# The exact rest of streamed weights, by a subtraction on VectorE or by an accumulating DMA

## The chip, the cores and the metric

The kernel runs on one core of one Trainium2 chip. The metric is the device time of one execution in microseconds (us); lower is better. A second number, the span, is the time from the first to the last instruction in one profiled execution.

## The reference

One layer of a hybrid decoder works on 512 prompt tokens and 32 sample tokens (8 sequences of 4), 1024 channels wide. After an RMSNorm comes one input projection for seven parts. A diagonal state-space branch (S5) and a gated linear recurrence (HGRN2, 8 heads) run side by side and are merged by sigmoid gates; then an output projection, and an MLP with a squared ReLU, each with norms around it:

```python
h = rms_norm(x, norm_mix_pre)
proj = h @ w_in + b_in                                   # 1024 -> 6656
u, q, f, i, g, gate_s5, gate_hg = jnp.split(proj, SPLIT_POINTS, axis=-1)
y_s5, s5_re, s5_im = s5_mixer(u, ...)
y_hg, hg_s = hgrn2_mixer(q, f, i, g, ...)
merged = jax.nn.sigmoid(gate_s5) * (y_s5 @ w_br_s5) + jax.nn.sigmoid(gate_hg) * (y_hg @ w_br_hg)
x = x + rms_norm(merged @ w_out, norm_mix_post)
h2 = rms_norm(x, norm_mlp_pre)
m = jnp.square(jax.nn.relu(h2 @ w_up)) @ w_down          # 1024 -> 4096 -> 1024
x = x + rms_norm(m, norm_mlp_post)
```

All inputs are fp32. The outputs are the tokens and the final states of both branches.

## The kernel before, in words

Channels lie on the 128 partitions, tokens along the rows: 544 tokens as two halves of 272. A dense product is done in three passes over fp32r operands: each operand is cut into a high part (11 bits of mantissa) and the exact rest, and TensorE sums high x high, high weight x rest of the activation, and rest of the weight x high. `dense` (L106) does this for one column tile of 128 outputs: per block k of 128 input channels it issues three pairs of matmuls, the two halves of the tokens each, in the order wh·xh, wh·xl, wl·xh. A tile of 8 blocks is 48 matmuls and reads weights of 128 x 1024 words (512 KB); a tile of w_down has 7 blocks, 42 matmuls and 128 x 896 words (448 KB).

`weights` (L83) brings in such a tile. SP's queue loads the fp32 words into wt (three buffers), ScalarE copies them into wh, which rounds them (L97), and VectorE subtracts wh from wt into wl (L98; as it goes through the helper tt, the profile shows it as L69). wh and wl have two buffers each in the pool wp. Where a caller passes a pool as `res`, the two parts get places of their own there and stay: four column tiles of w_out and four of w_up, which are used by halves of the tokens. Everything else is streamed: column tiles come in, are used once and make room. In the profile a streamed tile carries its matrix's name: wt_in, wh_in, wl_in for the input projection, _bh and _bs for the branches, _gl for the gated linear unit, _o for the output projection, _u and _d for the MLP.

The order of TensorE's work up to the branches is written out by hand: column tiles of the input projection are cut into blocks (`dense_steps`, class Fill) and put between the matmuls of the HGRN2 cores, the S5 tables and the S5 scan, a few blocks at a time. From about 530 us the kernel is mainly one column tile after another: gated linear unit, S5 branch, output projection, then the MLP in three parts (14 + 14 + 4 tiles of w_up; after each of the first two, 8 x 2 tiles of w_down). The last tiles of the output projection and the first of w_up are done by halves of the tokens, and the last 512 rows of w_down (w_down2) are cut into two parts by `split` (L129), outside of `weights`.

The order on the other engines comes from a scheduler that places instructions as it expects them to become ready, by their place in the program less an offset: weights run ahead by 100 (WAHEAD), the emptying of PSUM by 50 (EAHEAD). The head (up to `make_masks()`, where the tiles 4 and 5 of w_in are loaded early) and the tail are ordered by hand on TensorE, ScalarE and VectorE. All engines and queues work in their order. POOL's queue carries the constants, S5's loads (U, PT, tab, Q, T, L890 to L898), the stores y_d (L962) and some memsets.

What empties PSUM after a column tile: in the input projection a sigmoid or a copy on ScalarE (L501, L520, L974), in w_up a ReLU on ScalarE and then a square on VectorE, a copy and a subtraction (`act_full`, L1164 to L1168), in w_down a copy on ScalarE in the first part (L1217) and an addition on VectorE in the second (L1219).

Of the kernel before, what the change touches and what calls it, by code (L numbers as in the profile page):

```python
# [9 lines left out]
F32 = mybir.dt.float32  # L10
# [10 lines left out]
NT = 544          # tokens: two halves of 256 prompt + 16 sample tokens  # L21
# [4 lines left out]
WAHEAD, EAHEAD = 100, 50     # how far weights and the emptying of PSUM run ahead in the schedule  # L26
# [13 lines left out]
def b2(ap, n):  # L40
    """[p, a] -> [p, a, n], the last axis repeated."""
    return ap.unsqueeze(2).to_broadcast([ap.shape[0], ap.shape[1], n])
# [3 lines left out]
def layer(ctx, tc, a, o):  # L46
    nc = tc.nc
# [35 lines left out]
    def weights(src, name, res=None, ahead=WAHEAD):  # L83
        """res: a pool in which the two parts stay."""
        n = 1
        for d in src.shape[1:]:
            n *= d
        if len(src.shape) == 3:
            src = src.rearrange("p a b -> p (a b)")
        elif len(src.shape) == 4:  # L90
            src = src.rearrange("p a b c -> p (a b c)")
        with tc.high_priority(offset=ahead):
            wt = wp.tile([P, n], F32, tag="wt", name=f"wt_{name}", bufs=3)
            nc.sync.dma_start(out=wt, in_=src)
            wh = (res or wp).tile([P, n], F32R, tag="wh", name=f"wh_{name}")
            wl = (res or wp).tile([P, n], F32R, tag="wl", name=f"wl_{name}")
            S.copy(wh, wt)  # L97
            tt(wl, wt, wh.bitcast(F32), SUB)  # L98
        return wh, wl
# [6 lines left out]
    def dense(ps, wh, wl, xs, first=True, last=True):  # L106
        """ps[:, half, :] (+)= sum_k W_k^T X_k; xs: per k the halves of the hi and the lo part."""
# [8 lines left out]
    def dense_half(ps, ws, xs, hf, ks=None):  # L116
        """ps[:, i, :] = sum_k W_ik^T X_k for two column tiles i and one half of the tokens; ks: these k alone."""
# [16 lines left out]
    gains = const("gains", q=nc.gpsimd)        # [128, 4, 8]  # L134
    lg = const("lb_logits", q=nc.gpsimd)

    def rstd(r, q2, ps):
        """r = 1/sqrt(ps/1024), good to the last bits; ps: 1024 * (mean of squares + eps)."""
        S.activation(r, ps, AF.Abs_reciprocal_sqrt, bias=zero_t, scale=1.0 / 1024)
        S.activation(q2, r, AF.Square)  # L140
        stt(q2, ps, -0.5 / 1024, q2, MUL, MUL)
        stt(r, q2, 1.5, r, ADD, MUL)
# [67 lines left out]
    bmask = const("bmask", q=nc.gpsimd)          # [128, 8]  # L210
    hgn = const("hg_norm", q=nc.gpsimd)          # [128, 1]

    def hq(t):
        """[p, 2, 544] in halves -> prompt [p, 2, 256], sample [p, 2, 16]; t: [p, 2, >=272]"""
        return t[:, :, 0:256], t[:, :, 256:HT]

    def tq(t):
        """[p, 544] prompt first, sample last -> the same two views"""
# [13 lines left out]
    # the input and what goes into S5 lie where the next groups' tiles will  # L232
# [10 lines left out]
    # ---- first norm and the S5 input, half of the tokens after half; the input goes through DRAM to be laid out by  # L243
    # (step in chunk, channel) ----
# [11 lines left out]
    def sums0(hf):  # L256
# [3 lines left out]
        # each of 128 partitions adds its share of 1024 eps  # L260
# [67 lines left out]
    # lower bound of the forget gate: softmax over the two rows, first row  # L328
# [34 lines left out]
    with tc.manual_schedule(engines={ET.PE, ET.Activation, ET.DVE, ET.SP}):  # L363
        # the tensor engine's clock comes up while the first loads are under way
# [77 lines left out]
    def inproj(m):  # L442
        """One column tile of the input projection; yields after each of its 8 blocks of rows."""
# [12 lines left out]
    class Fill:  # L456
        """Column tiles that go into the tensor engine's stream a few blocks at a time, between other work."""
# [19 lines left out]
    # blocks of column tiles between the parts of the S5 tables, the HGRN2 cores and the S5 scan  # L477
    F1, F2, F3, FL, FK, FO, FN, FH, FY, FD, FS = 44, 1, 32, 5, 4, 2, 3, 22, 3, 12, 2

# [1 line left out]
    def hgrn_in(g, gp):  # L481
        """The tiles of a group of two heads and what fills them."""
# [42 lines left out]
    def hgrn_core(g, T, hp, scT, scS):  # L525
        """Scores inside windows of 128 tokens (4 for samples), level by level: blocks of 2h tokens, queries of the
        upper half against keys of the lower. qp: q times the decay since its block of h began; k: k times the decay
        until its block ends; tots: the decay of whole blocks. All factors are at most 1."""
# [10 lines left out]
        def lv(t, h, n):  # L539
            """blocks of 2h tokens as [p, d, n, 2, h], or with (d n) as one axis"""  # L540
# [7 lines left out]
        # token-major values and keys  # L548
# [25 lines left out]
        def sample_tokens():  # L574
            # samples: four copies of the 32 tokens along the rows, cut so that one pass sums all partial products
# [35 lines left out]
        for L in range(7):  # L611
# [19 lines left out]
            # on to blocks of 2h  # L631
# [25 lines left out]
        # states after each window, and the outputs  # L657
# [15 lines left out]
        for i in range(2):  # L673
            # token by token, so that the norm's sums run along the rows
# [12 lines left out]
        # the samples' outputs lie feature by feature  # L687
# [37 lines left out]
    y_d = dp.tile([8, 16, 32, 72], F32, tag="y_d", name="y_d")  # L725

    def cmul(e, outr, outi, xr, xi, yr, yi, t, conj=False):
        """out = x * y (or its conjugate); out aliases neither."""
# [21 lines left out]
    def s5_parameters(sp):  # L750
        """Per state: decay and rotation of a step and of a chunk, and the input coefficient."""
# [7 lines left out]
        # decay per step and per chunk of 8 steps; rotation per 1, 8, 16, .., 256 steps  # L759
# [31 lines left out]
        # input coefficient (A - 1) / a  # L791
# [12 lines left out]
    def s5_tables(sp, keep):  # L804
        """The large tables, which depend on the parameters alone, into DRAM."""
# [8 lines left out]
        # -Im C, and C in blocks for pairs of groups  # L814
# [11 lines left out]
        # rotation tables  # L826
# [18 lines left out]
        # the response inside a chunk  # L845
# [12 lines left out]
        # what a chunk adds to the state  # L858
# [10 lines left out]
        # read-out of the state t+1 steps on  # L869
# [12 lines left out]
    def s5_late(sp, keep):  # L882
# [3 lines left out]
        for hf in range(2):  # L886
# [25 lines left out]
            # sample states  # L912
# [17 lines left out]
            # the states before each chunk, for pairs of groups in blocks  # L930
# [9 lines left out]
            for c in range(4):  # L940
# [11 lines left out]
                # gelu: y * sigmoid(2 sqrt(2/pi) (y + 0.044715 y^3))  # L952
# [138 lines left out]
    def squares(acc, ps, name, first):  # L1091
        """acc += ps^2, [128, 2, n] each"""
# [8 lines left out]
    with tc.tile_pool(name="res", bufs=5, reuse_waits="tile") as rp:  # L1101
# [53 lines left out]
        def act_out(ps, dst, n):  # L1155
            """relu(ps)^2 into the two parts of each dst"""
# [13 lines left out]
        # relu(r x)^2 = r^2 relu(x)^2: the norm's factor r = 1/sqrt(v) is left out before the MLP; with it the  # L1170
        # last norm's 1/sqrt(mean + eps) is 1/sqrt(mean + eps v^2) of what comes out. e8: eps v^2, as what
        # each of 128 partitions adds to the sum over 1024 channels
# [20 lines left out]
    with tc.tile_pool(name="act", bufs=1, reuse_waits="tile") as apool:  # L1193
# [26 lines left out]
        # the last part's weights stay, in the place of activations that are done  # L1220
# [17 lines left out]
        def e_out(m, hf):  # L1238
            """Adds the parts, squares; the gain comes in after the squares."""
# [66 lines left out]
def kperm(w, k):  # L1306
    """[k*128, m*128] -> [m, 128, k, 128]"""
# [72 lines left out]
```

## Time and profile before

| | |
|---|---|
| median of 2 runs | 1028.97 us (1028.68 to 1029.27) |
| span of the profiled execution | 1027.5 us |
| instructions | 18826 |
| TensorE busy | 1010.4 us, 98% of the span |
| VectorE busy | 550.1 us, 54% |
| ScalarE busy | 399.9 us, 39% |
| POOL busy | 40.5 us, 4% |
| moved by the DMA queues | 107.27 MB, 104 GB/s on average |

The profiled execution is known by its span alone; the runs, timed without a profile, are 1.2 to 1.8 us above it. PE is TensorE's matmuls, PEld its weight loads (beside PE), DVE VectorE, ACT ScalarE, SP the queue that issues most DMAs. Matmuls overlap, so the length of one (288 ns) is more than the distance from one to the next; the pace of the stream is read from starts. PEclk is the granted clock as a share of full speed.

### The profile page before, as it was taken

Reading aid. Unit: us, or ns where it says so; the run is one execution under the profiler, and the core shown is the slowest. Engines: PE = TensorE matmul, PEld = TensorE weight load, DVE = VectorE, ACT = ScalarE, POOL = GpSimd, SP = SyncE. Lnnn points to the kernel's source line nnn. Section 1 sums busy time; section 2 is a strip of 40 time slices with the busy share of each in tenths; the row PEclk is TensorE's granted clock in tenths of the full one; section 3 lists DMA queues with packets and bytes.
Section 4 is the critical chain, followed back from the end, with each engine's and each line's share of the span. In section 5 each row is a group of like instructions: output and inputs, shape, how many; then the busy total and the mean of one; then the engine's idle time right before and its main releaser. Section 6 shows DMA issues by size and latency. Waiting matters only on the chain.

```text
span 1027.5 us, 18826 instructions
## 1 busy us (share of the span) xinstructions
PE 1010.4 (98%) x8032; PEld 993.7 (97%) x8032; DVE 550.1 (54%) x1006; ACT 399.9 (39%) x740; POOL 40.5 (4%) x77
## 2 busy tenths in 40 slices
PE   8999999999999999999999999999999999999995
PEld 6999999999999999999999999999999999999994
DVE  7856447466465496767547649445211344322357
ACT  6654254253442633344324546343222333211243
POOL 1100000000000000124110000000000000000000
PEclk9999899999999999999999999999999999999998
DMA  7431132131131243845452341122233222222312
GB/s 266 102 120 48 56 108 83 45 126 62 58 127 58 89 141 131 290 138 207 149 152 83 103 144 63 41 81 73 90 91 100 83 87 91 75 88 93 107 38 88
DMA packets 37796, 107.27 MB, mean 104 GB/s; under 512 B 8320, under 2 KB 11744, under 8 KB 37200
## 3 DMA queue, kind: packets, MB, share of 16 engines
q1 hardware_dynamic: 33440, 91.82, 27.8%
q0 software_dynamic: 3728, 13.68, 4.1%
q8 instruction: 63, 1.03, 0.4%
q10 hardware_dynamic: 544, 0.56, 0.2%
q14 instruction: 21, 0.17, 0.1%
HBM read 90.04 MB, written 14.83 MB: 102 GB/s over the span
## 4 chain that ended last, share of the span: by engine, by line
PE 95%; DVE 2%; ACT 1%; DMA 1%; SPq 0%; issue 0%; DVEq 0%; ACTq 0%
PE ps_in L114 27%; PE ps_d L114 16%; PE ps_u L114 15%; PE ps_u L124 7%; PE ps_bh L114 5%; PE psL L619 5%; PE ps_o L114 2%; PE ps_o L124 2%; PE ps_bs L114 2%; PE ps_e L124 2%; PE psOs L596 1%; PE psy L950 1%; DMA wt_in<-in_w_in 1%; PE psD L608 1%; PE psO L679 1%; PE psK L663 1%
## 5 line engine op out<-in xcount | busy, mean ns | idle before, releaser
L114 PE MATMUL ps_in<-hh,wh_in 128*128 128x272 f32 x736 | 159.8, 298 | 0.0
L114 PE MATMUL ps_in<-hh,wl_in 128*128 128x272 f32 x736 | 154.2, 291 | 0.0
L114 PE MATMUL ps_in<-hl,wh_in 128*128 128x272 f32 x736 | 154.1, 290 | 0.0
L114 PEld LDWEIGHTS ps_in<-hh,wh_in 128*128 128x128 f32 x736 | 117.0, 191 | 0.9
L114 PEld LDWEIGHTS ps_in<-hl,wh_in 128*128 128x128 f32 x736 | 117.1, 191 | 0.0
L114 PEld LDWEIGHTS ps_in<-hh,wl_in 128*128 128x128 f32 x736 | 116.8, 191 | 0.0
L69 DVE TENSOR_TENSOR wl_in<-wt_in,wh_in 128x1024 fp32r<-128x1024 f32 (+1 forms) x54 | 61.6, 1143 | 66.1 <-ACT wh_in L97 64.4
L97 ACT CAST wh_in<-wt_in 128x1024 fp32r<-128x1024 f32 x46 | 48.3, 1051 | 118.9 <-PE ps_in L114 105.0
L114 PE MATMUL ps_u<-zl,wh_u 128*128 128x272 f32 x416 | 86.3, 289 | 0.0
L114 PE MATMUL ps_u<-zh,wh_u 128*128 128x272 f32 x416 | 86.1, 288 | 0.0
L114 PE MATMUL ps_u<-zh,wl_u 128*128 128x272 f32 x416 | 86.0, 288 | 0.0
L69 DVE TENSOR_TENSOR wl_d<-wt_d,wh_d 128x896 fp32r<-128x896 f32 x32 | 35.0, 1092 | 93.8 <-ACT wh_d L97 93.7
L97 ACT CAST wh_d<-wt_d 128x896 fp32r<-128x896 f32 x32 | 30.1, 942 | 123.6 <-PE ps_d L114 113.2
L69 DVE TENSOR_TENSOR wl_u<-wt_u,wh_u 128x1024 fp32r<-128x1024 f32 x32 | 39.0, 1224 | 71.3 <-ACT wh_u L97 71.2
L114 PEld LDWEIGHTS ps_u<-zh,wh_u 128*128 128x128 f32 x416 | 65.4, 188 | 0.2
L114 PEld LDWEIGHTS ps_u<-zh,wl_u 128*128 128x128 f32 x416 | 65.4, 188 | 0.0
L114 PEld LDWEIGHTS ps_u<-zl,wh_u 128*128 128x128 f32 x416 | 65.1, 189 | 0.0
L97 ACT CAST wh_u<-wt_u 128x1024 fp32r<-128x1024 f32 x32 | 33.4, 1047 | 70.2 <-PE ps_u L114 46.6
L114 PE MATMUL ps_d<-a0l,wh_d 128*128 128x272 f32 x256 | 53.1, 289 | 0.0
L114 PE MATMUL ps_d<-a0h,wl_d 128*128 128x272 f32 x256 | 52.9, 288 | 0.0
L114 PE MATMUL ps_d<-a0h,wh_d 128*128 128x272 f32 x256 | 52.8, 288 | 0.0
L619 PE MATMUL psL<-qp,k 128*128 128x64 f32 (+2 forms) x448 | 52.1, 268 | 0.0
(477 smaller groups left out, 2129.6 us busy)
## 6 DMA issues: line engine op xcount, KB each, us to landing
wt_in<-in_w_in SPq DMA_DIRECT2D x52, 512.0 KB, 3.6
wt_u<-in_w_up SPq DMA_DIRECT2D x32, 512.0 KB, 3.4
wt_d<-in_w_down SPq DMA_DIRECT2D x32, 448.0 KB, 3.3
s<-in_hg_s SPq DMA_DIRECT2D x8, 512.0 KB, 4.9
out_hg_s<-s SPq DMA_DIRECT2D x8, 512.0 KB, 3.4
wt_bh<-in_w_br_hg SPq DMA_DIRECT2D x8, 512.0 KB, 3.5
wt_o<-in_w_out SPq DMA_DIRECT2D x8, 512.0 KB, 3.4
x<-in_x POOLq DMA_DIRECT2D x2, 1088.0 KB, 8.7
```

The lines of the kernel that those rows point to most:

```text
L69: (e or V).tensor_tensor(out=out, in0=x, in1=y, op=op)
L97: S.copy(wh, wt)
L114: mm(ps[:, i, 0:int(np.prod(x[i].shape[1:]))], lhsT=w[:, c], rhs=x[i], start=st, stop=sp)
L124: mm(ps[:, i, 0:HT], lhsT=ws[i][j][:, c], rhs=x[hf], start=st, stop=sp)
L596: mm(pos[:, 4 * b:4 * b + 4], lhsT=s0[:, b], rhs=qp[:, i, NP_ + 4 * b:NP_ + 4 * b + 4], start=False, stop=(b == 7))
L608: mm(pd[:, w], lhsT=k[:, i, c], rhs=q[:, i, c], start=True, stop=True)
L619: mm(pq[0:m, i, w * 64:(w + 1) * 64], lhsT=k[:, i, w * P:w * P + m], rhs=up(w * P, (w + 1) * P, i), start=True, stop=True)
L663: mm(pk[:, w], lhsT=kt2[:, i, w], rhs=vt[:, i, w], start=True, stop=True)
L679: mm(po[:, w], lhsT=sc[:, i, c], rhs=vt[:, i, w], start=True, stop=(w == 0))
L950: mm(py2[:, 72 * x_:72 * x_ + 72], lhsT=T.rearrange("p t c g -> p (t c) g")[:, :, 2 * gp_ + x_], rhs=U[:, 2 * gp_ + x_, 0:72], start=False ...
```

## The change

For streamed weights (no `res`) VectorE's subtraction goes. In its place ScalarE writes the negated high part into wl, and a DMA on POOL's queue reads the same weights from DRAM again and adds them onto wl, so that wl holds the weights less their high part. Resident weights keep the subtraction. Apart from this the diff only takes out comments.

```diff
             S.copy(wh, wt)
-            tt(wl, wt, wh.bitcast(F32), SUB)
+            if res is None:
+                S.activation(wl, wh.bitcast(F32), AF.Copy, scale=-1.0)
+                nc.gpsimd.dma_start(out=wl, in_=src, accum_op=ADD)
+            else:
+                tt(wl, wt, wh.bitcast(F32), SUB)
         return wh, wl
```

## Rows read from the trace of the kernel before

**Rows 1.** The page: span, and busy us, share and instructions of each engine.
```profile
span 1027.5 us, 18826 instructions
PE 1010.4 (98%) x8032; PEld 993.7 (97%) x8032; DVE 550.1 (54%) x1006; ACT 399.9 (39%) x740; POOL 40.5 (4%) x77
```
**Rows 2.** Stretches: length; busy us of PE, PEld, DVE, ACT, POOL; PEclk; DMA share; GB/s.
```profile
0.00:50.00 50.00, 46.39 (x297) 39.96 (x297) 37.72 (x125) 31.82 (x70) 7.23 (x24) 1.00 0.58 182
...
660.00:950.00 290.00, 290.00 (x2309) 289.84 (x2308) 96.07 (x108) 83.38 (x110) 0.00 (x0) 1.00 0.27 84
950.00:1027.50 77.50, 65.47 (x507) 63.84 (x506) 42.36 (x68) 28.68 (x51) 0.00 (x0) 0.95 0.24 77
```
**Rows 3.** Timeline of PE around tiles of w_up: start, length, engine, line, operation.
```profile
819.62 0.41 PE L114 MATMUL ps_u<-zh,wh_u 128*128 128x272 f32 x2
...
825.64 0.41 PE L114 MATMUL ps_u<-zh,wh_u 128*128 128x272 f32 x2
...
826.14 0.41 PE L114 MATMUL ps_u<-zh,wl_u 128*128 128x272 f32 x2
```
**Rows 4.** The same around tiles of w_down.
```profile
763.87 0.41 PE L114 MATMUL ps_d<-a0h,wh_d 128*128 128x272 f32 x2
...
769.14 0.41 PE L114 MATMUL ps_d<-a0h,wh_d 128*128 128x272 f32 x2
...
769.64 0.41 PE L114 MATMUL ps_d<-a0h,wl_d 128*128 128x272 f32 x2
```
**Rows 5.** Timeline of ACT there, w_up; in brackets idle time before and its releaser.
```profile
819.61 1.05 ACT L97 CAST wh_u<-wt_u 128x1024 fp32r<-128x1024 f32 x1 [2.40 <-PE ps_u L114]
820.56 0.62 ACT L1166 ACTIVATE t_u<-ps_u 128x544 f32<-128x544 f32 x1
```
**Rows 6.** The page, groups: count | busy us, mean ns | idle before, releaser.
```profile
L69 DVE TENSOR_TENSOR wl_d<-wt_d,wh_d 128x896 fp32r<-128x896 f32 x32 | 35.0, 1092 | 93.8 <-ACT wh_d L97 93.7
L69 DVE TENSOR_TENSOR wl_u<-wt_u,wh_u 128x1024 fp32r<-128x1024 f32 x32 | 39.0, 1224 | 71.3 <-ACT wh_u L97 71.2
...
L97 ACT CAST wh_u<-wt_u 128x1024 fp32r<-128x1024 f32 x32 | 33.4, 1047 | 70.2 <-PE ps_u L114 46.6
```
**Rows 7.** Timeline of ACT, w_down.
```profile
763.82 0.94 ACT L97 CAST wh_d<-wt_d 128x896 fp32r<-128x896 f32 x1 [4.33 <-PE ps_d L114]
764.66 0.61 ACT L1217 COPY ov<-ps_d 128x544 f32<-128x544 f32 x1
```
**Rows 8.** DMA issues: count, KB each, median us from issue to landing.
```profile
wt_u<-in_w_up SPq DMA_DIRECT2D x32, 512.0 KB, 3.4
...
x<-in_x POOLq DMA_DIRECT2D x2, 1088.0 KB, 8.7
...
PT<-pt_d POOLq DMA_DIRECT2D x2, 1024.0 KB, 6.0
...
sb<-in_s_b POOLq DMA_DIRECT2D x1, 256.0 KB, 2.9
```
**Rows 9.** Timeline of ACT: first and last close wh copies, two of the looser ones.
```profile
64.01 1.05 ACT L97 CAST wh_in<-wt_in 128x1024 fp32r<-128x1024 f32 x1 [3.18 <-PE ps_in L114]
...
123.25 1.05 ACT L97 CAST wh_in<-wt_in 128x1024 fp32r<-128x1024 f32 x1 [2.80 <-PE ps_in L114]
...
131.43 1.05 ACT L97 CAST wh_in<-wt_in 128x1024 fp32r<-128x1024 f32 x1 [1.37 <-PE ps_in L114]
...
970.31 1.05 ACT L97 CAST wh_u<-wt_u 128x1024 fp32r<-128x1024 f32 x1
```
**Rows 10.** Timeline of POOL: two of its waits.
```profile
414.32 0.54 POOL L893 DMA_DIRECT2D PT<-pt_d  x1 [47.03 <-DMA pt_d<-pb]
...
518.89 0.54 POOL L962 DMA_DIRECT2D y_d<-ysb  x1 [21.77 <-DVE ysb L69]
```

## The prediction

> **What bounds the kernel now.** I read the busy shares first: TensorE is busy for 1010.4 of 1027.5 us, VectorE for half, ScalarE for 39% [rows 1]. Then the stretches, to see where the remaining 17.1 us are [rows 2]: 3.6 us fall into the first 50 us and 12.0 us into the last 77.5, and from 660 to 950 us TensorE has no idle time at all and a granted clock of 1.00 (its 2.4 GHz level). So the kernel is bound by the stream of matmuls, and nothing that only empties another engine can gain more than a trifle. What matters is whether the weights still come in time.
>
> So I read the pace of the stream. One streamed weight tile of 1024 words lasts from 819.62 to 825.64 us, 6.02 us, and its first matmul on the rest wl comes 0.50 us after its start, at 826.14 for the next tile [rows 3]. A w_down tile of 896 words lasts from 763.87 to 769.14, 5.27 us, and the next one needs its rest at 769.64 [rows 4].
>
> There are two buffers for wh and two for wl. Tile t+2 can be cut only when tile t is done, and must be ready when tile t+1 is done: the whole preparation has one tile's time, about 6 us. Before the change it takes little of that: ScalarE's wh copy starts 0.01 us before tile t+1 does [rows 5] (it waits for the last use of wh, one pair before the end) and takes 1.05 us, VectorE's subtraction 1.22 us [rows 6]. Ready after some 2.3 us, needed after 6.5: over 4 us in hand.
>
> **The change part by part.** Counted from the code, 124 tiles are streamed: 46 of w_in, 8 of w_br_hg, 2 of w_glu, 4 of w_br_s5, 4 of w_out, 28 of w_up (92 of 1024 words), and 32 of w_down (896 words).
>
> Removed: 124 subtractions on VectorE, 92 x 1.22 + 32 x 1.09 = 147 us by [rows 6]. Gain: none. The rows say what VectorE waited for before them (ScalarE's wh, 71.2 us before wl_u alone), and TensorE had nothing to wait for in the stretches where they lie.
>
> Added on ScalarE: 124 negated copies of the same shapes as the wh copies: 92 x 1.05 + 32 x 0.94 = 127 us [rows 6, 7]. ScalarE goes from 399.9 to about 527 us, half of the span; hidden as work, but it stands in the chain. In w_up tiles a 0.62 us activation that empties PSUM starts right behind the wh copy [rows 5]; both become ready when tile t ends, and the order goes by place in the program less an offset: the negation stands some 60 instructions later with an offset of 100, the activation has 50. So I put the negation behind it. In w_down tiles a 0.61 us copy stands there for every second tile [rows 7].
>
> Added on POOL's queue: 124 DMAs that read the weights a second time, add them to what lies in wl, and write it. POOL issues little else after 530 us. SP's loads into wt come a little earlier, as wt is now free after the wh copy.
>
> The new chain, 1024 words, from the start of tile t+1 (819.62): wh copy to 820.66, PSUM activation to 821.18, negation (started 0.1 us before that ends, as in [rows 5]) to 822.13, POOL's issue begins at about 822.2. Needed at 826.14. So 3.95 us are left for the DMA from issue to landing. For 896 words: wh copy from 763.82 to 764.76, negation to 765.6, or 766.1 where the PSUM copy is in front; needed at 769.64: 4.0 or 3.5, mean 3.75 us.
>
> What the DMA takes, L: the trace has no accumulating DMA, so bounds. Below: a plain 512 KB load by SP lands in 3.4 us; a plain one by POOL, interpolated between 256 KB in 2.9 and 1024 KB in 6.0, in 3.9 us [rows 8]. That would just be hidden. The nearest row for the true one: the add reads 512 KB from DRAM and 512 KB from wl, 1024 KB of reading, and POOL's 1024 KB load landed in 6.0 us (median). Above: 8.7 us, POOL's 1088 KB load beside other traffic [rows 8]; here SP's next 512 KB load runs at the same time. I take 6.0, and 5.5 for w_down (the same slope of 0.5 us per 128 KB of reading).
>
> The Trainium skill speaks against the change at this point: "Collectives: The Full Stack", section "The bandwidth ceiling: the fold count and why AG ≠ RS ≠ AR", says that an add in the DMA path costs rate not through the arithmetic but because it reads two sources, which halved the rate it measured. With the fixed 2 us plus bytes over 436 GB/s of "DMA: Bandwidth & Descriptors" (section on the anatomy of one DMA), a megabyte of reading gives an estimate of 4.4 us, and a sum of about 1056 us by the steps below. No row here shows an add; the 1024 KB row of 6.0 is slower than that fit.
>
> The stall. wl of tile t+2 is late by L minus the time left, but a stall in tile t+1 itself pushes the need of t+2 back by as much. In a steady row of tiles the stalls of two neighbours add up to L minus the time left, so one tile stalls by half: (6.0 - 3.95)/2 = 1.03 us for 1024 words, (5.5 - 3.75)/2 = 0.88 for 896.
>
> How many tiles. From the starts of the wh copies along the whole trace: 83 follow each other within 7 us (51 of 1024 words, 32 of w_down; the first at 64.01, the last at 970.31 [rows 9]), with nothing between the tiles to hide a stall. The other 41 stand further apart, mostly in the HGRN2 cores, where other matmuls lie between; the close ones among them are 8.2 us apart [rows 9], which leaves 3.95 + 2.2 = 6.15 us: hidden at L = 6.0. Sum: 51 x 1.03 + 32 x 0.88 = 52 + 28 = 80 us.
>
> The queue that the DMAs are put into. POOL works in order. From 366 to 527 us it waits in its own queue for others: 47.0 us before the load of PT, 21.8 before a store of y_d [rows 10], and two more waits above 5 us. An accumulation placed behind such a wait starts late although its data is ready. Bounds: nothing, if all stand in front; 9 us for each of the four (a tile and half of the next) if they stand behind. I take 2.5 each, 10 us, since the program's order follows expected readiness.
>
> The rest: the two early tiles add 2.1 us to ScalarE's hand-written order near 40 us; the second reading of 63 MB (92 x 0.524 + 32 x 0.459) is no bound, as the DMA engines' share is 0.27 in the dense stretch [rows 2]. Both at zero; without cover the first costs its 2.1 us.
>
> Sum: 1027.5 + 80 + 10 = 1117.5 us of span. The two runs have a median of 1028.97, 1.5 us above the profiled span; with that, **1119 us**.
>
> **The rivals.**
> A. The DMA is fast enough (not slower). Place: the landing in wl. Point: L up to 3.95 us costs nothing; up to 4.5 us costs (0.55/2) x 51 + about 0.18 x 32 = 20 us, 1049. For it: the plain 512 KB interpolates to 3.9 us, and the DMA engines are three quarters idle. Against: it must also read what it adds to, and every plain POOL row of that amount is at 6.0 or more. Time 1029 to 1049.
>
> B. The DMA is much slower, L = 8.7: (8.7 - 3.95)/2 = 2.38 x 51 = 121, (8.2 - 3.75)/2 = 2.23 x 32 = 71, and now about 13 of the looser tiles stall by (8.7 - 6.15)/2 = 1.3, 17 us; with POOL's 10, 1248 us. For it: read, add and write may not overlap as a copy does, and SP's load shares the engines. Against: nothing in the trace beyond the 8.7 row. Gaps in TensorE may also cost clock: the last stretch, with 12.0 idle of 77.5 us, has 0.95 granted on average between its two levels [rows 2]. 5% over the 475 us of the dense tiles is 24 us; it is inside the range, and I don't add it, since 1 us gaps are short beside those.
>
> C. POOL's queue decides: the accumulations stand behind its waits, 9 us x 4 = 36 in place of 10: 1145 us. Against: the order is planned by readiness.
>
> D. The relief of VectorE shows (faster): in the parts where VectorE is on the chain TensorE idles 17.1 us in all, 15.6 of it in the head and the tail, where no streamed weight is cut. At most 1.5 us: 1027 us.
>
> **How the numbers follow.** L between 4.5 and 7.2 us (1049 to about 1175): 0.50; B, L above that: 0.26; C: 0.08; A: 0.14; faster, by something that I don't see: 0.02. Two per cent (20.6 us) is about what a measurement of this kernel tells from no change. A lies within it; the forecast, B and C are slower. The range for 8 in 10 leaves out most of A at the bottom and a DMA above L = 8.7 at the top: 1040 to 1245 us. The time is that of the likeliest case, 1119.
>
> **What would show it.** Right: the accumulating DMA lands in about 6 us; TensorE idles before its first matmul on wl of a tile, ended by that DMA, about 1 us for each of some 83 tiles, between 660 and 980 us about 51 us in all; wh copies in the dense part are 7.0 and 6.2 us apart on average; VectorE loses 147 us and ScalarE gains 127. A step is wrong if the landing is under 4.5 us (then nothing happens), if the PSUM activation comes after the negation (0.6 us more in hand), if TensorE waits for ScalarE rather than for the DMA, or if POOL's DMAs wait long for a semaphore other than ScalarE's. The whole is wrong if TensorE shows no idle time at wl.

## The result, and the profile after

The changed kernel takes 1171.4 us (median of 2 runs, 1169.61 and 1173.2), the kernel before 1028.97. The ratio is 1.1386 with a 95% interval of 1.1343 to 1.1428, so it is slower by 142 us, where the prediction had 90. The direction and the place were right; the size has two parts that the sum did not hold, the stalls ahead of the MLP and a longer busy time of TensorE, and they are followed up below. In the lines of after, the numbers of the code lie 4 higher (L114 is now L118); the negation is L99, the accumulating DMA L100.

The page of after: the span, the busy shares and the software queue. These lines answer to [rows 1]:

```profile
span 1167.8 us, 19072 instructions
PE 1049.3 (90%) x8032; PEld 1017.6 (87%) x8032; DVE 412.6 (35%) x882; ACT 514.5 (44%) x864; POOL 146.2 (13%) x201
...
q0 software_dynamic: 21584, 76.60, 34.8%
```

VectorE lost 124 instructions and 137.5 us, ScalarE gained 124 and 114.6 us. Both are some 10 us less than the 147 and 127 that were counted from single durations, since neighbouring instructions of an engine overlap by about 0.1 us and busy time counts that once. TensorE's idle time rose from 17.1 to 118.5 us, by 101.4. Its busy time, for the same 8032 matmuls, rose from 1010.4 to 1049.3, by 38.9. The two make up the span's 140.3.

What TensorE idled for stands in the groups of after's page (count, busy us, mean ns, then idle time before the group and its releaser), and beside it the DMA issues (count, KB, median us from issue to landing):

```profile
L118 PE MATMUL ps_in<-hh,wl_in 128*128 128x272 f32 x736 | 158.4, 298 | 31.3 <-DMA wl_in<-in_w_in 31.3
...
L118 PE MATMUL ps_u<-zh,wl_u 128*128 128x272 f32 x416 | 88.4, 294 | 17.9 <-DMA wl_u<-in_w_up 17.9
...
L118 PE MATMUL ps_d<-a0h,wl_d 128*128 128x272 f32 x256 | 56.5, 302 | 26.7 <-DMA wl_d<-in_w_down 26.6
...
wl_in<-in_w_in POOLq DMA_DIRECT2D x46, 512.0 KB, 5.3
...
wl_u<-in_w_up POOLq DMA_DIRECT2D x28, 512.0 KB, 5.1
...
wl_d<-in_w_down POOLq DMA_DIRECT2D x32, 448.0 KB, 5.3
...
wl_bh<-in_w_br_hg POOLq DMA_DIRECT2D x8, 512.0 KB, 7.5
```

The matmuls on wl wait, and for the accumulating DMA, not for ScalarE or VectorE. These three groups hold 75.9 us of the idle time, the one of w_br_hg another 13.4.

Where in the kernel it happens is seen best by stage. Each window below runs from a stage's first matmul to the next stage's (columns as in [rows 2]): the HGRN2 cores with the input projection; the S5 scan with w_br_hg; w_glu to the halves of the output projection and of w_up; the streamed MLP. First the kernel before:

```profile
52.00:393.60 341.60, 341.19 (x2752) 334.01 (x2751) 199.74 (x430) 141.16 (x311) 3.78 (x9) 0.98 0.26 86
393.60:538.70 145.10, 145.10 (x1212) 144.61 (x1211) 89.50 (x144) 53.39 (x96) 29.48 (x44) 1.00 0.55 184
538.70:662.00 123.30, 122.20 (x966) 121.39 (x965) 82.82 (x124) 61.49 (x104) 0.00 (x0) 1.00 0.29 90
662.00:988.40 326.40, 326.40 (x2599) 326.24 (x2598) 113.03 (x129) 96.16 (x129) 0.00 (x0) 1.00 0.28 86
```

And the same four stages after:

```profile
52.20:425.90 373.70, 349.82 (x2752) 340.49 (x2751) 159.49 (x372) 172.84 (x346) 33.07 (x43) 0.96 0.53 131
425.90:607.80 181.90, 156.37 (x1213) 153.99 (x1212) 66.06 (x118) 71.05 (x114) 46.17 (x63) 0.93 0.70 196
607.80:742.10 134.30, 125.70 (x966) 123.01 (x965) 69.47 (x111) 74.07 (x117) 10.94 (x13) 0.99 0.54 135
742.10:1128.80 386.70, 342.18 (x2599) 332.80 (x2598) 51.31 (x73) 146.41 (x185) 47.13 (x56) 0.99 0.64 143
```

The stages grew by 32.1, 36.8, 11.0 and 60.3 us. Head and tail, with two accumulations in the head and none in the tail, kept their length to 0.2 us. The number of matmuls in a stage is the same to one, so the first two numbers of a row split each growth: idle time +23.5, +25.5, +7.5, +44.5, and busy time +8.6, +11.3, +3.5, +15.8.

One cycle of the w_up tiles shows the mechanism. ScalarE's timeline (start, length, operation, in brackets idle time before and its releaser), which answers to [rows 5]:

```profile
902.82 1.05 ACT L97 CAST wh_u<-wt_u 128x1024 fp32r<-128x1024 f32 x1 [3.72 <-PE ps_u L118]
903.77 0.62 ACT L1170 ACTIVATE t_u<-ps_u 128x544 f32<-128x544 f32 x1
904.29 1.05 ACT L99 ACTIVATE wl_u<-wh_u 128x1024 fp32r<-128x1024 f32 x1
```

POOL's there:

```profile
905.63 0.85 POOL L100 DMA_DIRECT2D wl_u<-in_w_up  x1 [5.40 <-ACT wl_u L99]
912.96 0.84 POOL L100 DMA_DIRECT2D wl_u<-in_w_up  x1 [6.48 <-ACT wl_u L99]
```

And TensorE's, around two matmuls that waited (answering to [rows 3]):

```profile
903.12 0.41 PE L118 MATMUL ps_u<-zl,wh_u 128*128 128x272 f32 x2
904.56 0.52 PE L118 MATMUL ps_u<-zh,wl_u 128*128 128x272 f32 x2 [1.03 <-DMA wl_u<-in_w_up]
904.92 0.42 PE L118 MATMUL ps_u<-zh,wh_u 128*128 128x272 f32 x2
...
918.14 0.52 PE L118 MATMUL ps_u<-zh,wl_u 128*128 128x272 f32 x2 [1.25 <-DMA wl_u<-in_w_up]
```

The PSUM activation stands ahead of the negation, as forecast. The negation ends at 905.34 and POOL begins to issue at 905.63, 2.81 us after the cycle began at 902.82. The DMA issued at 912.96 lands about 5.1 us later, and TensorE goes on at 918.14. Between the two stalls lies a tile without one: two tiles share the lack, and it falls on every second one.

Not all gaps are that short. Here is one of the longer ones, in TensorE's timeline:

```profile
960.81 0.78 PE L118 MATMUL ps_u<-zh,wl_u 128*128 128x272 f32 x2 [3.30 <-DMA wl_u<-in_w_up]
...
962.29 0.66 PE L118 MATMUL ps_u<-zh,wl_u 128*128 128x272 f32 x2
```

and the windows of 2 us around it (third number from the end: granted clock):

```profile
960.00:962.00 2.00, 1.19 (x5) 1.19 (x6) 0.59 (x1) 0.00 (x0) 0.44 (x1) 0.72 0.62 150
962.00:964.00 2.00, 2.00 (x11) 2.00 (x10) 0.00 (x0) 0.00 (x0) 0.00 (x0) 0.50 1.03 195
964.00:966.00 2.00, 2.00 (x17) 2.00 (x16) 0.00 (x0) 0.00 (x0) 0.00 (x0) 0.93 0.07 12
```

After 3.3 us without work the granted clock is 0.50, the 1.2 GHz level, and comes back to 1.00 by 966 us. In between a pair of matmuls takes 0.66 us instead of 0.41. Such a gap thus costs more than its length.

### The profile page after: what moved, and what is told of

Its sections match the earlier page's. It is cut to its first block, busy times and chain, and to the rows that moved or that the text cites. A ratio compares the mean times of both kernels' runs of the same rounds, so it can differ in the third digit from the quotient of the medians.

```text
span 1167.8 us, 19072 instructions
## 1 busy us (share of the span) xinstructions
PE 1049.3 (90%) x8032; PEld 1017.6 (87%) x8032; DVE 412.6 (35%) x882; ACT 514.5 (44%) x864; POOL 146.2 (13%) x201
## 3 DMA queue, kind: packets, MB, share of 16 engines
q8 instruction: 63, 1.03, 0.3%
## 4 chain that ended last, share of the span: by engine, by line
PE 53%; DMA 22%; issue 18%; ACT 2%; DVE 2%; POOL 2%; SPq 0%; POOLq 0%; DVEq 0%; ACTq 0%
PE ps_in L118 18%; PE ps_u L118 9%; DMA wl_in<-in_w_in 6%; PE ps_u L128 6%; DMA wl_u<-in_w_up 6%; DMA wl_d<-in_w_down 4%; PE psL L623 4%; PE ps_d L118 3%; PE ps_o L128 2%; PE ps_o L118 2%; PE ps_e L128 2%; DMA wl_bh<-in_w_br_hg 1%; PE psOs L600 1%; DMA Q<-q_d 1%; DMA wl_o<-in_w_out 1%
## 5 line engine op out<-in xcount | busy, mean ns | idle before, releaser
L118 PE MATMUL ps_in<-hh,wl_in 128*128 128x272 f32 x736 | 158.4, 298 | 31.3 <-DMA wl_in<-in_w_in 31.3
L118 PE MATMUL ps_in<-hh,wh_in 128*128 128x272 f32 x736 | 162.5, 303 | 0.0
L118 PE MATMUL ps_in<-hl,wh_in 128*128 128x272 f32 x736 | 156.2, 294 | 0.0
L118 PEld LDWEIGHTS ps_in<-hh,wl_in 128*128 128x128 f32 x736 | 119.2, 195 | 34.1 <-DMA wl_in<-in_w_in 34.1
L118 PEld LDWEIGHTS ps_in<-hh,wh_in 128*128 128x128 f32 x736 | 119.9, 196 | 0.9
L118 PEld LDWEIGHTS ps_in<-hl,wh_in 128*128 128x128 f32 x736 | 119.6, 195 | 0.0
L118 PE MATMUL ps_u<-zh,wl_u 128*128 128x272 f32 x416 | 88.4, 294 | 17.9 <-DMA wl_u<-in_w_up 17.9
L69 DVE TENSOR_TENSOR t_u<-t_u 128x544 f32<-128x544 f32 x32 | 23.2, 725 | 224.2 <-ACT t_u L1170 213.4
L100 POOL DMA_DIRECT2D wl_in<-in_w_in x46 | 39.1, 851 | 405.9 <-ACT wl_in L99 288.9
L118 PE MATMUL ps_u<-zh,wh_u 128*128 128x272 f32 x416 | 87.0, 290 | 0.0
L118 PE MATMUL ps_u<-zl,wh_u 128*128 128x272 f32 x416 | 86.7, 289 | 0.0
L118 PEld LDWEIGHTS ps_u<-zh,wl_u 128*128 128x128 f32 x416 | 65.5, 190 | 21.1 <-DMA wl_u<-in_w_up 20.9
L118 PE MATMUL ps_d<-a0h,wl_d 128*128 128x272 f32 x256 | 56.5, 302 | 26.7 <-DMA wl_d<-in_w_down 26.6
L97 ACT CAST wh_u<-wt_u 128x1024 fp32r<-128x1024 f32 x32 | 33.6, 1049 | 103.6 <-PE ps_u L118 72.9
L118 PEld LDWEIGHTS ps_d<-a0h,wl_d 128*128 128x128 f32 x256 | 40.0, 190 | 32.7 <-DMA wl_d<-in_w_down 32.5
L118 PEld LDWEIGHTS ps_u<-zh,wh_u 128*128 128x128 f32 x416 | 66.0, 190 | 0.2
L118 PEld LDWEIGHTS ps_u<-zl,wh_u 128*128 128x128 f32 x416 | 65.7, 190 | 0.0
L118 PE MATMUL ps_d<-a0h,wh_d 128*128 128x272 f32 x256 | 53.0, 288 | 0.0
L118 PE MATMUL ps_d<-a0l,wh_d 128*128 128x272 f32 x256 | 53.0, 288 | 0.0
```

The source lines that it names most:

```text
L69: (e or V).tensor_tensor(out=out, in0=x, in1=y, op=op)
L100: nc.gpsimd.dma_start(out=wl, in_=src, accum_op=ADD)
L118: mm(ps[:, i, 0:int(np.prod(x[i].shape[1:]))], lhsT=w[:, c], rhs=x[i], start=st, stop=sp)
```

## The experiments

The theory after the result (called theory 1 in the expectations): with two places each for wh and wl, the whole chain of copy, negation, issue and landing has one tile's time; it takes longer, and half of the lack shows at each tile. Its rivals were throughput (the DMA engines or POOL's queue are too slow for the doubled reading), the load on ScalarE, and the traffic beside the accumulations. Experiments 1, 4, 6, 7, 8, 11 and 12 are one run each; the kernel before ranged from 1027.85 to 1034.15 us in 14 runs, so a few us between single runs say nothing.

**1. The negation without the DMA.** The DMA is replaced by an addition on VectorE; the negation on ScalarE stays.

```diff
-                nc.gpsimd.dma_start(out=wl, in_=src, accum_op=ADD)
+                tt(wl, wt, wl.bitcast(F32), ADD)
```

> ScalarE's negated copy stays, VectorE adds wt onto it instead of the DMA. Theory 1 (the DMA's landing is too long for the one tile's time that two places of wl leave): the chain is 1.05 + 0.62 + 1.05 + 1.2 = 3.9 us against 6.5, so TensorE does not idle at wl and the time is that of before, 1029 us (1025 to 1035). Theory 2 (the DMA engines cannot carry the second reading): also 1029. Theory 3 (the negation on ScalarE, in front of other work, is what delays): stays above 1100.

Measured: 1037.94 us, beside 1030.57 for the kernel before on the same chip. The span is 1036.2, and from 660 to 990 us TensorE has next to no idle time:

```profile
660.00:990.00 330.00, 329.91 (x2625) 329.53 (x2624) 113.84 (x131) 148.46 (x189) 0.00 (x0) 1.00 0.28 87
```

So the 124 negations cost at most some 7 us, slightly more than expected, and the rest, 133 us, comes with the DMA.

**2. A third place for wl alone.** wt and wl share five places.

```diff
-            wt = wp.tile([P, n], F32, tag="wt", name=f"wt_{name}", bufs=3)
+            wt = wp.tile([P, n], F32, tag="wt", name=f"wt_{name}", bufs=5)
...
-            wl = (res or wp).tile([P, n], F32R, tag="wl", name=f"wl_{name}")
+            wl = res.tile([P, n], F32R, tag="wl", name=f"wl_{name}") if res else wp.tile([P, n], F32R, tag="wt", name=f"wl_{name}", bufs=5)
...
```

> wl and wt share five places, so that wl of a tile can be prepared while two others are in use or ready. Theory 1: the chain gets up to two tiles' time, 12 us against about 8; TensorE's idle time at wl falls from about 100 us to under 20 and the time to 1030 to 1060, with the landing still at 5 us or more. Theory 2: the DMA engines are as loaded, 1140 or more.

Measured: 1177.91 us, ratio 1.1367 (1.1284 to 1.145), not to be told from the change: a miss. The reason is in the timeline of ScalarE in this run:

```profile
904.95 1.05 ACT L97 CAST wh_u<-wt_u 128x1024 fp32r<-128x1024 f32 x1 [4.11 <-PE ps_d L118]
...
906.41 1.06 ACT L99 ACTIVATE wl_u<-wh_u 128x1024 fp32r<-128x1024 f32 x1
```

The wh copy still waits for TensorE, as wh has only two places, and the negation reads wh. A third place for one of two tiles that are made in a row brings nothing. Experiment 5 mends that.

**3. The DMA in two halves.**

```diff
-                nc.gpsimd.dma_start(out=wl, in_=src, accum_op=ADD)
+                for c_ in (slice(0, n // 2), slice(n // 2, n)):
+                    nc.gpsimd.dma_start(out=wl[:, c_], in_=src[:, c_], accum_op=ADD)
```

> The accumulating DMA in two of half the columns each. Theory 1: the first matmul on wl needs the first half alone, which should land in about 3.9 us (5.3 less half of some 2.9 us of engine time); with 0.3 us from the negation to POOL's issue about 0.3 us are missing, 0.15 a tile: 1040 to 1070 us, if a matmul waits for its half alone. Theory 2: same bytes, 1150 or more.

Measured: 1132.0 us, ratio 1.096 (1.0898 to 1.1022). About 39 of the 142 us come back, not the 100 and more that were expected. The DMA issues, two to a tile, and below them one pair in the timelines of POOL and TensorE:

```profile
wl_u<-in_w_up POOLq DMA_DIRECT2D x56, 256.0 KB, 5.1
...
wl_d<-in_w_down POOLq DMA_DIRECT2D x64, 224.0 KB, 5.3
```

```profile
783.27 1.72 POOL L101 DMA_DIRECT2D wl_d<-in_w_down  x2 [5.18 <-ACT wl_d L99]
...
787.26 0.49 PE L119 MATMUL ps_d<-a0h,wl_d 128*128 128x272 f32 x2 [0.60 <-DMA wl_d<-in_w_down]
```

These medians of 5.1 and 5.3 us mix the two halves of a tile. POOL begins their issues 0.54 us apart and they run together; taken by themselves, the first halves landed 4.4 us (w_up) and 4.3 us (w_down) after their issue in the median, the second halves 5.4 and 5.5. A matmul does wait for its half alone: at 787.26 TensorE goes on 3.99 us after the pair's issue at 783.27, when the second half, which landed at 789.35, is still under way. So the first matmul on wl gained 0.7 to 1.0 us and not the 1.2 to 1.4 that 3.9 us would have given; TensorE's idle time in the streamed MLP fell from 44.5 to 25.3 us. Theory 1 held in kind, with a half that lands later than was put down for it.

**4. The same DMA without the addition.** It overwrites wl with the weights themselves, so the subtraction is left out of the result; negation, queue and bytes read from DRAM are as in the change.

```diff
-                nc.gpsimd.dma_start(out=wl, in_=src, accum_op=ADD)
+                nc.gpsimd.dma_start(out=wl, in_=src)
```

> The DMA doesn't add: wl gets the weights themselves, a plain 512 KB load behind the same negated copy (the subtraction is left out of the computation). Tells what the adding costs: a plain POOL load should land in about 3.9 us where the adding one takes 5.3, which leaves about 0.2 us a tile missing: 1040 to 1070 us by theory 1. If the time is still above 1120, the place behind the negation costs more than the adding.

Measured: 1113.79 us, far above what was expected. Span, software queue, and the landing of the plain load:

```profile
span 1112.0 us, 19072 instructions
...
q0 software_dynamic: 21584, 76.60, 23.6%
...
wl_u<-in_w_up POOLq DMA_DIRECT2D x28, 512.0 KB, 4.3
```

So even a plain load by POOL, behind copy and negation, lands too late, and costs 76 us more than experiment 1; the addition costs the last 58. It lengthens the landing from 4.3 to 5.1 us. In time on the DMA engines it is dearer: an accumulating DMA takes (0.348 x 1167.8 - 0.041 x 1027.5)/124 = 2.94 us of all 16 engines, a plain one (0.236 x 1112.0 - 42.1)/124 = 1.78 (the subtracted part is the software queue of the kernel before, 42.1 us). That is a factor of 1.65.

**5. A third place for wh and wl.** wt, wh and wl share seven places, the same memory as before.

```diff
-            wt = wp.tile([P, n], F32, tag="wt", name=f"wt_{name}", bufs=3)
+            wt = wp.tile([P, n], F32, tag="wt", name=f"wt_{name}", bufs=7)
...
-            wh = (res or wp).tile([P, n], F32R, tag="wh", name=f"wh_{name}")
-            wl = (res or wp).tile([P, n], F32R, tag="wl", name=f"wl_{name}")
+            wh = res.tile([P, n], F32R, tag="wh", name=f"wh_{name}") if res else wp.tile([P, n], F32R, tag="wt", name=f"wh_{name}", bufs=7)
+            wl = res.tile([P, n], F32R, tag="wl", name=f"wl_{name}") if res else wp.tile([P, n], F32R, tag="wt", name=f"wl_{name}", bufs=7)
...
```

> wt, wh and wl share seven places in place of 3 + 2 + 2: now wh too can have a third place, which the run with a third place of wl alone lacked (its negation still waited for wh, whose two places come free with the tile). Theory 1 (the chain from the end of tile t to the landing doesn't fit into one tile's time): the chain gets up to two tiles' time, TensorE's idle time at wl falls under 20 us and the time to 1030 to 1060. Theory 2 (the DMA engines or POOL's queue can't carry the second reading at this pace): 1130 or more.

Measured: 1051.34 us, ratio 1.0203 (1.017 to 1.0235). The S5 stage and the streamed MLP of this run, and its landing:

```profile
400.00:560.00 160.00, 145.75 (x1174) 143.60 (x1174) 65.03 (x118) 68.39 (x110) 45.17 (x62) 0.96 0.81 221
...
680.00:1010.00 330.00, 329.97 (x2626) 329.60 (x2624) 49.27 (x71) 144.61 (x184) 47.55 (x56) 1.00 0.79 172
...
wl_u<-in_w_up POOLq DMA_DIRECT2D x28, 512.0 KB, 5.4
```

One of its w_down tiles shows what the further places did:

```profile
893.31 0.94 ACT L97 CAST wh_d<-wt_d 128x896 fp32r<-128x896 f32 x1 [2.98 <-PE ps_u L118]
...
905.91 0.41 PE L118 MATMUL ps_d<-a0h,wl_d 128*128 128x272 f32 x2
```

The copy is made 12.60 us ahead of the first matmul on wl, about twice what such a tile has in the change.

This is the run that settles it for the dense tiles. The same DMAs move the same bytes, land no sooner (5.4 us), and keep the DMA engines busier (0.79 instead of 0.64, as the stage is shorter), and in the streamed MLP TensorE has no idle time left. What cost the time there was the latency inside one tile's time, not the throughput of the DMA engines, of POOL or of ScalarE. About 120 of the 142 us are gone. What is left, some 22 us, is mostly in the S5 stage, which has 14 us idle of 160; its longest wait, 6.1 us, is no longer at a wl but for the load of PT, which stands in POOL's queue too.

**6. The change for w_down alone.**

```diff
-            if res is None:
+            if res is None and name[0] == "d":
```

> The accumulating DMA for the 32 tiles of w_down alone, all others by VectorE. Theory 1: a stall of about 1.0 us a tile as in the changed kernel and nothing elsewhere: 1029 + 32 to 42 = 1061 to 1071 us. If the clock that TensorE loses were a matter of the whole kernel and not of the gaps, it would also be slow before 700 us.

Measured: 1070.23 us, as expected by adding tiles up. The two groups of w_down tiles, and the w_up tiles between them:

```profile
712.00:812.00 100.00, 86.64 (x649) 83.35 (x648) 2.68 (x3) 32.92 (x40) 12.69 (x15) 0.98 0.66 141
812.00:897.00 85.00, 85.00 (x679) 85.00 (x678) 33.71 (x39) 31.11 (x42) 0.52 (x1) 1.00 0.28 90
897.00:997.00 100.00, 85.76 (x646) 82.79 (x645) 6.53 (x9) 29.40 (x32) 13.09 (x16) 0.98 0.68 141
```

Of these stretches only those with accumulations have idle time, 13.4 and 14.2 us for 16 tiles each: 0.86 a tile. The rest of the 40 us is busy time: TensorE was busy for 1021.4 us, 11.0 longer than before the change. Ahead of 700 us it lost nothing (646.49 of the 648 us from 52 us on are busy, at a granted clock of 0.99, as before), so the lost clock belongs to the gaps and not to the kernel as a whole.

**7. Without w_in and w_br_hg.**

```diff
-            if res is None:
+            if res is None and name[:2] not in ("in", "bh"):
```

> The accumulating DMA for all streamed weights but w_in and w_br_hg. Theory 1, stages that add up: before the gated linear unit the time of before (to about 539 us), behind it the loss of the changed kernel there, 4.8 + 6.3 + 60.3 = 71 us: 1100 us. A rival, that the losses come from POOL's and the DMA queues' backlog carried over from the S5 stage, would give less behind it, under 1080.

Measured: 1109.6 us. Up to 540 us the kernel runs like the one before (487.60 of 488 us busy). So the 54 tiles of w_in and w_br_hg cost some 62 us (the two stages grew by 69), where the prediction had 34 for all 64 tiles ahead of the streamed MLP, POOL's queue included, and the loss is local in the main: the rival, that later stages pay for a backlog of the S5 stage, wanted less than 1080 us. The time is 10 us above the 1100 that were expected, as the stages behind lost some 80 us here and not 71; in a single run this was not followed up.

**8. The negation on VectorE**, to take the PSUM activation and 0.4 us of copying out of the chain.

```diff
-                S.activation(wl, wh.bitcast(F32), AF.Copy, scale=-1.0)
+                ts(wl, wh.bitcast(F32), -1.0, MUL)
```

> The negation goes to VectorE, the DMA stays. It then runs beside ScalarE's activation that empties PSUM, so the chain gets 0.6 us shorter in w_up and in every second tile of w_down, and by what VectorE is faster than ScalarE's 1.05 us. Theory 1: half of each us taken out of the chain comes back per dense tile, 0.3 to 0.6 us x 83: 1120 to 1147 us. Theory 2 (throughput of DMA or POOL): no change, 1165 to 1175.

Measured: 1206.35 us: both theories missed. POOL did issue earlier, in w_down tiles with a PSUM copy 1.89 us after the wh copy's start (884.40 to 886.29) instead of 2.60 (846.52 to 849.12). But the landing grew by about as much:

```profile
wl_u<-in_w_up POOLq DMA_DIRECT2D x28, 512.0 KB, 6.1
...
wl_d<-in_w_down POOLq DMA_DIRECT2D x32, 448.0 KB, 5.9
```

What it could be: SP's plain load into wt starts as soon as the wh copy is done, so an earlier accumulation runs beside it for longer. Experiments 11 and 12 try that.

**9 and 10. Seven places before the change, and with it from w_glu on.** A control, and what is left of the loss with three places for wh and wl. Experiment 9 is the kernel before with the places of experiment 5; experiment 10 is experiment 5 with the condition of experiment 7.

> The kernel before (the subtraction on VectorE) with the seven shared places for wt, wh and wl of the earlier run: a control for it. Theory 1 (the chain before fitted into one tile's time with over 4 us in hand, so the third place buys nothing there): 1025 to 1033 us, ratio within 1% of one. Rival (the order in which the shared places come round delays loads or the places by themselves gain something): under 1020, or over 1036 us, and then the 1051 of the change with seven places must be read against that.

> Seven shared places, and the accumulating DMA for all streamed weights but w_in and w_br_hg (these keep VectorE's subtraction), so 70 of 124 tiles. Theory 1 (what is left of the loss with seven places, some 22 us, lies in the HGRN2 cores and the S5 stage, where the accumulations meet the other traffic, and the dense tiles from w_glu on are free with three places): 1028 to 1036 us. Rival (the loss is spread over all tiles, or is the doubled reading itself): 1039 to 1048 us.

Measured: 1033.86 us for the control, ratio 1.0045 (1.0024 to 1.0067), and 1032.03 us for the DMA in 70 of 124 tiles, ratio 1.0022 (1.0007 to 1.0037). By both theory 1 holds, though the control lies just above its 1033 us. The third place buys nothing where the chain fits, and with it the dense tiles pay nothing for the DMA; its MLP stage has 329.97 us busy of 330. So some 19 of the 22 us that were left in experiment 5 (1051.34 less 1032.03) belong to w_in and w_br_hg, in the HGRN2 cores and the S5 stage. No version was faster than the kernel before.

**11 and 12. Without the plain load beside it.** For the 32 w_down tiles SP's load into wt is replaced by a constant from VectorE, so that wh no longer comes from the weights; 11 has ScalarE's negation, 12 VectorE's.

```diff
-            nc.sync.dma_start(out=wt, in_=src)
+            if res is None and name[0] == "d":
+                nc.vector.memset(wt, 0.01)
+            else:
+                nc.sync.dma_start(out=wt, in_=src)
```

> The change, but for the 32 w_down tiles SP's first load into wt is left out (VectorE fills wt with a constant), so that the accumulating DMA runs without a plain load of 448 KB beside it; this leaves the true weights out of wh, and the output isn't the reference's. The question is why the landing is 5.1 to 5.4 us for 512, 448, 256 and 224 KB alike. Theory X (it shares the DMA engines with SP's load of the next tile): wl_d lands in at most 4.5 us instead of 5.3, TensorE's idle time before wl_d falls from 26.7 to under 12 us, total 1140 to 1157 us. Theory Y (a time of its own, whatever runs beside): wl_d lands in 5.0 us or more, idle time 22 to 28 us, total 1163 to 1177 us.

> The same with the negation on VectorE, where wl_d landed in 5.9 us with the load beside it. There the accumulation is issued about 0.9 us after SP's load, with ScalarE's negation about 1.8 us after it. Theory X (the longer landing is the larger overlap with SP's load): wl_d lands within 0.2 us of what it takes in the run with ScalarE's negation and no load, so at most 4.7 us, and the total falls from 1206 by 25 us or more. Theory Y (the negation by VectorE itself makes the landing longer, or a fixed time): wl_d lands in 5.6 us or more and the total stays above 1190 us.

Measured: 1161.62 and 1158.13 us (the kernel before beside them 1025.94). Landing of the w_down tiles in experiment 11, and below it of w_up and w_down in experiment 12:

```profile
wl_d<-in_w_down POOLq DMA_DIRECT2D x32, 448.0 KB, 5.0
```

```profile
wl_u<-in_w_up POOLq DMA_DIRECT2D x28, 512.0 KB, 6.0
...
wl_d<-in_w_down POOLq DMA_DIRECT2D x32, 448.0 KB, 5.0
```

An accumulation of 448 KB takes 5.0 us even with no load beside it, and TensorE's idle time before wl_d is 24.5 us: theory Y in experiment 11, though the total is 1 us under its range. What lies on top is the load: 0.3 us with ScalarE's negation, where the accumulations of w_down are issued 1.2 to 1.7 us after it, and 0.9 with VectorE's, where most are issued 0.93 us after it. In experiment 12 the landing of w_down is the same with either engine's negation, though w_up, whose loads were left in, stays at 6.0. So VectorE's negation itself lengthens nothing; its lead is eaten by the overlap. That accounts for experiment 8 gaining nothing in the dense tiles. Why experiment 8 came out 35 us above the change is only partly explained: its TensorE was busy for 1073.7 us, at a granted clock of 0.943 on average, and what made its gaps longer in the first half was not tried.

## Why the prediction was right, and what it mis-sized

**What bounds the kernel** was right: the stream of matmuls and, beside it, one tile's time for the preparation of a tile. The relief of VectorE was worth nothing (rival D), and experiment 5 shows the one-tile limit directly.

**The chain up to the issue** was nearly right. The order on ScalarE was the one predicted, the issue came 2.81 us after the cycle's start instead of 2.58. The missing 0.2 is between the end of the negation and POOL's issue, 0.29 us where the sum had 0.07. That left 6.52 - 2.81 = 3.71 us for the DMA instead of 3.95.

**The landing** was over-sized: 5.1 us for w_up and 5.3 for w_down instead of 6.0 and 5.5. The bound from [rows 8] that counted what is read (1024 KB by POOL in 6.0 us) was nearer than the plain 512 KB in 3.9, but too high, and the step to 448 KB by a slope was wrong: those landed no sooner. Rival A's point, a landing under 4.5 us, was not reached; experiment 4 shows that a plain load at 4.3 us, inside what rival A had between 3.95 and 4.5 at 1049 us at most, already costs 1113.79. The estimate of 4.4 us that the prediction made with the Trainium skill ("DMA: Bandwidth & Descriptors", on the anatomy of one DMA) was too low by 0.7. What the Trainium skill says in "Collectives: The Full Stack" (section on the bandwidth ceiling), that reading a second source halved the rate it measured, points the right way: the runs here show 1.65 times the engine time for the addition, less than a doubling.

**Half of the lack per tile** held. For w_up (5.1 - 3.71)/2 = 0.70 us a tile; the idle time is 17.9/28 = 0.64. For w_down, with the same 0.2 us later issue, (5.3 - 3.55)/2 = 0.87; measured 26.7/32 = 0.83. Experiment 4 fits it too: with a landing of 4.3 us half of the lack makes 28 x 0.30 + 32 x 0.38 = 20 us, and TensorE idled for 6.4 us before wl_u and 14.0 before wl_d. In sum these 60 tiles were put at 28 x 1.03 + 32 x 0.88 = 57 us of idle time, and the streamed MLP shows 44.5.

**The tiles before the MLP** were under-sized. The prediction had 23 other dense tiles at 1.03 us and 10 us for POOL's queue, 34 us; the other three stages show 23.5 + 25.5 + 7.5 = 56.5 us of idle time. The step that failed is "The other 41 stand further apart ... hidden at L = 6.0". It took the distance between two wh copies for the time that a tile has in hand, and one L for the whole kernel. In TensorE's timeline the HGRN2 stage has only 9 stalls at wl, but 6 of them are longer than 2 us and make up 20.1 of 22.6 us; in the S5 stage 6 of 8 make up 19.7 of 22.1.

The time in hand runs from a tile's own copy to its own first matmul on wl. Here is a tile whose copy stands 14.43 us behind the one before it; first in the kernel before:

```profile
358.14 1.04 ACT L97 CAST wh_in<-wt_in 128x1024 fp32r<-128x1024 f32 x1
...
363.23 0.41 PE L114 MATMUL ps_in<-hh,wl_in 128*128 128x272 f32 x2
```

and the same tile after:

```profile
377.30 1.04 ACT L97 CAST wh_in<-wt_in 128x1024 fp32r<-128x1024 f32 x1
...
379.73 0.84 POOL L100 DMA_DIRECT2D wl_in<-in_w_in  x1 [13.10 <-ACT wl_in L99]
...
386.51 0.52 PE L118 MATMUL ps_in<-hh,wl_in 128*128 128x272 f32 x2 [3.94 <-DMA wl_in<-in_w_in]
```

Already before the change wl was needed 5.09 us after the copy, less than the 6.5 us of a dense tile, for all the distance between the copies. After it the issue comes 2.43 us after the copy, and a landing of 5.3 us would have been some 2.5 us late. Four tiles of w_in, with copies 14 to 18 us behind the one before, had 5.1 to 6.1 us in hand in the kernel before; these stall for 2.52, 3.45, 4.90 and 3.94 us in the changed one (at 67.42, 226.39, 305.55 and 386.51), 14.8 of the stage's 22.6 us.

Besides, several accumulations landed later than the median: 8.0 and 8.1 us after the issues at 218.33 and 297.40, beside stores and loads of states, 6.8 after the one at 379.73, 8.6 after the one at 549.84. In the windows of 2 us from 302 to 310 us the DMA engines' share is 0.98 to 1.09. The one behind the stall at 67.42 landed in 5.1 us, so there the short time in hand alone is the cause; for the others the two causes were not separated. The term for POOL's waits (rival C) was not what decided: before the accumulations of w_in POOL waited for ScalarE's negation in 288.9 of 405.9 us. Some did stand behind a wait of the queue, as the one at 585.90 behind a load of yt that had waited 3.10 us for the store of y_d; how much each added was not separated.

**The clock** was left out of the sum: "24 us; it is inside the range, and I don't add it, since 1 us gaps are short beside those". For the 1 us gaps that was right; between 796 and 888 us, with stalls of up to 1.33 us, the granted clock stays at 1.00. But the gaps at wl of more than 2 us, 12 of 17 of them in the HGRN2 cores and the S5 stage, were not foreseen. The mean granted clock fell from 0.989 to 0.968. Over the spans that is 0.032 x 1167.8 - 0.011 x 1027.5 = 26 us of full speed, part of it in idle time.

**The edges of a stall** were in no term either. Around the stall at 904.56 pairs of matmuls last 0.41 us and follow each other by 0.25; the pair of 903.12 has nothing to overlap its last 0.16 us, and the pair at 904.56 is followed by the next after 0.36 us, 0.11 late. So this stall of 1.03 us delays the stream by 1.30. An estimate from this one for all 61 stalls at wl is 61 x 0.27 = 16 us. With the clock's 26 us, less what of it fell into idle time, that can account for the 38.9 us by which TensorE's busy time grew; in experiment 6 the same sum is 27 x 0.27 = 7 us and 3 us of clock, for 11.0 measured.

So the 140 us of span are 101 of idle time, where 90 were predicted from a landing that was too long in the dense tiles and too little idle time before them, and 39 of longer busy time, where nothing was in the sum. That the idle time came out within 12 us of the forecast is in part luck, as its two errors (12.5 us too much for the streamed MLP, 22.5 too little before it) have opposite signs.

## What to carry to other kernels

Before moving a short step of a preparation chain onto a DMA, count the time from the release of the buffer to the need of the next tile, and set the whole chain against it, issue and landing included; half of the lack per tile is a good first sum for two buffers. A further place helps only if every tile of the chain gets one. Count that time for each tile from its own copy to its own first use, not from the distance between copies, and take the landing for each stage with its own traffic rather than one median. Price a stall with its edges, and gaps of several microseconds with the clock that TensorE loses after them.

## What was not expected of the hardware

An accumulating DMA from POOL has a long time of its own: 448 KB took 5.0 us with no plain load beside it, and of two halves of 256 KB, issued 0.54 us apart, the first took 4.4 and the second 5.4 (experiment 3). Issuing it took POOL 0.84 us, a plain one 0.53 (experiment 4). Issuing it up to 0.7 us earlier, closer behind the plain load, brought no gain, since the landing of w_down grew by 0.6 and that of w_up by 1.0 (experiment 8).

The granted clock did not answer to the length of a gap alone. After idle times of 2.46 us (at 770.79) and 2.52 us (at 67.42) it stayed at 1.00; after 2.37 us (at 1015.59) and 2.25 us (at 1094.08) a window of 2 us at 0.50 followed (1016 to 1018 and 1094 to 1096 us). What sets the two kinds apart was not tried.
